# A softplus polynomial moved to GpSimd, the low mask products to ScalarE, and whole-chunk low halves on VectorE, in a two-layer hybrid decoder

## The chip, the cores and the metric

One Trainium2 chip, one of its cores. The metric is the device time of one execution in microseconds (us); the number given for a kernel is the median of several runs. Engines: TensorE (PE, its weight loads PEld), VectorE (DVE), ScalarE (ACT), GpSimd (POOL) and SyncE (SP), which issues the DMAs. Each engine takes its instructions strictly in the order in which they stand in its own queue.

## The reference

Two decoder layers on 256 tokens of width 1024 in float32. Each has a mixer (gated DeltaNet heads beside block attention heads, one output projection), a layer norm, a gated MLP with a causal convolution of width 3, and a layer norm. The part that the change touches is the log decay of the DeltaNet heads and how it becomes a decay matrix:

```python
beta = jax.nn.sigmoid(b_logit.astype(f32)).transpose(0, 2, 1)
g = (-jnp.exp(a_log.astype(f32)) * jax.nn.softplus(a_logit.astype(f32) + dt_bias.astype(f32))).transpose(0, 2, 1)
...
g = jnp.cumsum(g, axis=-1)
decay = jnp.exp(jnp.where(lower_incl, g[..., :, None] - g[..., None, :], -jnp.inf))
a_strict = jnp.where(idx[:, None] > idx[None, :],
                     jnp.einsum('bhncd,bhnmd->bhncm', k_beta, k) * decay, 0.0)
t_mat = a_strict + jnp.eye(c, dtype=q.dtype)
sol = lax.linalg.triangular_solve(t_mat, rhs, left_side=True, lower=True, unit_diagonal=True)
```

## The kernel before, in words

**Weights.** Every projection reads weights in chunks of 128x1024 float32. `load_raw` brings a chunk into one of 6 raw buffers `wr`. `split` makes two float32r halves of it: ScalarE copies the rounded high half `wh` (two 512-wide ops, L196), VectorE, or POOL where `le=pool`, subtracts it to get the low half `wl` (two 512-wide ops, L197). There are 5 buffers of each half. `proj` then runs 16 matmuls with the high half (L211 with the activations' high part, L212 with their low part) and 8 with the low half (L214) into a PSUM tile `pj`, of which there are two.

**A convolution chunk** (`u_conv`, names ka, qa, va): after `proj`, ScalarE scales `pj` by the last tap (L424), VectorE adds three taps from `pj` (L427, forms 255, 254, 253), ScalarE takes a tanh, VectorE forms the silu (L430). The `pj` tile is free for another chunk only after the last of the three VectorE taps. A rotary chunk (qb, kb) frees its `pj` by a ScalarE copy (L447).

**The decay.** `u_ab` projects the decay and beta logits, `u_ab2` (L390 to L418) forms y, beta, and the softplus as a chain of 128x8 operations: e = exp(-|y|), sd = e/(2+e) by a reciprocal, and a polynomial in sd squared, all on VectorE after the two exponentials. It ends in g, split into g_h and g_l, and in four products of a 128x512 triangular mask with them, `gx`: two with g_h on VectorE, two with g_l on POOL (L418). `u_decay` (L458 to L471) turns these by matmuls and exponentials into the decay matrices E0 and E1. `u_kk` and `u_sk` give k.k and its norms, `u_am` builds the matrix A on VectorE (L505, L507), which goes through DRAM to `u_solve`, a triangular solve of 28 small dependent POOL operations (L527, L529) and one copy, and back through DRAM to `gX` on VectorE (L543), which TensorE needs next (L560). `u_rp` adds the rotary part on POOL (L455, L456).

**Order.** The text table ORDER lists units (ab, ka:0, decay, ...) for each layer and, after @, engines on which a unit must stand after the one before it. Within these rules a scheduler with its own costs puts every engine's instructions in a fixed order. So an instruction that waits holds everything behind it on its engine.

**The MLP** runs for 22 column blocks of 128 two up-projection chunks and one down chunk of 128x1024 (12 matmuls of 512 columns); of the low halves of its up-projection, VectorE makes one chunk and POOL the other.

Of the kernel before, what the change touches and what calls it, by code (L numbers as in the profile page):

```python
# [11 lines left out]
F32 = mybir.dt.float32  # L12
F32R = mybir.dt.float32r
# [3 lines left out]
AF = mybir.ActivationFunctionType  # L17
OP = mybir.AluOpType
# [7 lines left out]
HG = 4  # L26
# [63 lines left out]
def hybrid_kernel(ctx, tc, xT, x, wab, wch, par, lnrow, cst, msk, out):  # L90
    nc = tc.nc
    pe, act, dve, pool, sp = nc.tensor, nc.scalar, nc.vector, nc.gpsimd, nc.sync
# [29 lines left out]
    def ps_a():  # L122
        return ac.tile([128, 512], F32, name="ac")
# [4 lines left out]
    m_le = kt[:, K_LE:K_LE + 128]  # L128
# [44 lines left out]
    def bc(ap, n):  # L173
        return ap[:, None, :].to_broadcast([128, n, 128])

    hold = {}
    nosync = mybir.DependencyInfo(mybir.DependencyClass.NoSync, mybir.DependencyReason.DATA)
# [6 lines left out]
    def split(raw, hp=None, le=None, tiles=None, cs=slice(0, 1024)):  # L184
        le = le or dve
        if tiles:
            h, lo = tiles
        elif hp is None:
            h = whp.tile([128, 1024], F32R, name="wh")
            lo = wlp.tile([128, 1024], F32R, name="wl")  # L190
        else:
            h = hp.tile([128, 1024], F32R, name="whh", bufs=N_HOLD)
            lo = hp.tile([128, 1024], F32R, name="wlh", bufs=N_HOLD)
        for q in range(cs.start, cs.stop, 512):
            s = slice(q, q + 512)
            ih = act.activation(h[:, s], raw[:, s], AF.Copy)  # L196
            il = le.tensor_tensor(lo[:, s], raw[:, s], h[:, s].bitcast(F32), op=OP.subtract)  # L197
            for i, e in ((ih, "act"), (il, "dve" if le is dve else "pool")):
                if e in hold:
                    tc.add_manual_dep(i.ins, hold[e].name, nosync, reason="norm first")  # L200
        return h, lo

    def load_chunk(l, ci, hp=None, le=None):
        return split(load_raw(l, ci), hp, le)
# [136 lines left out]
    for l in range(DEPTH):  # L341
# [5 lines left out]
        sh = [128, 2, HG]  # L347

        def sm(name):
            return small.tile(sh, F32, name=name, bufs=1)  # L350

        def mt(name, shape, bufs=1, dt=F32):
            return (early if name in EARLY else mix).tile(shape, dt, name=name, bufs=bufs)
# [4 lines left out]
        y, beta, ay, e, sd, s2, pl, g = (sm(n) for n in ("y", "beta", "ay", "e", "sd", "s2", "pl", "g"))  # L358
        sk, cj, ncj, rk, sq, so, wv = (sm(n) for n in ("sk", "cj", "ncj", "rk", "sq", "so", "wv"))
        g_h = small.tile(sh, F32R, name="g_h", bufs=1)  # L360
        g_l = small.tile(sh, F32R, name="g_l", bufs=1)
# [13 lines left out]
        G, T, st = [], {}, {}  # L375
# [15 lines left out]
        def u_ab2():  # L391
            ps = ps_a()
            for b in range(2):
                pe.matmul(ps[:, b * 8:b * 8 + 8], st["ab"][:, b * 128:b * 128 + 128], sel, start=True, stop=True)
            psv = ps[:, 0:16].rearrange("p (b c) -> p b c", b=2)
            dve.tensor_tensor(y, psv[:, :, 0:HG], pr[:, P_DT:P_DT + HG][:, None, :].to_broadcast(sh), op=OP.add)
            act.activation(beta, psv[:, :, HG:2 * HG], AF.Tanh, scale=0.5)
            dve.tensor_scalar(beta, beta, 0.5, 0.5, op0=OP.mult, op1=OP.add)
            dve.scalar_tensor_tensor(ay, y, -1.0, y, op0=OP.mult, op1=OP.max)
            act.activation(e, ay, AF.Exp, scale=-1.0)  # L400
            ea = small.tile([128, HG], F32, name="ea", bufs=1)
            act.activation(ea, pr[:, P_AL:P_AL + HG], AF.Exp)
            dve.tensor_scalar(sd, e, 2.0, None, op0=OP.add)
            dve.reciprocal(sd, sd)
            dve.tensor_tensor(sd, sd, e, op=OP.mult)
            dve.tensor_tensor(s2, sd, sd, op=OP.mult)
            dve.tensor_scalar(pl, s2, 2.0 / 17, None, op0=OP.mult)
            for n in (15, 13, 11, 9, 7, 5, 3):
                dve.scalar_tensor_tensor(pl, pl, 2.0 / n, s2, op0=OP.add, op1=OP.mult)
            dve.scalar_tensor_tensor(pl, pl, 2.0, sd, op0=OP.add, op1=OP.mult)  # L410
            dve.scalar_tensor_tensor(pl, y, 0.0, pl, op0=OP.max, op1=OP.add)
            dve.scalar_tensor_tensor(g, pl, -1.0, ea[:, None, :].to_broadcast(sh), op0=OP.mult, op1=OP.mult)
            dve.tensor_copy(g_h, g)
            dve.tensor_tensor(g_l, g, g_h.bitcast(F32), op=OP.subtract)
            for gg, eng in ((g_h, dve), (g_l, pool)):
                G.append(mt("gx", [128, 2, HG, 128], 2, F32R))
                for b in range(2):
                    eng.tensor_tensor(G[-1][:, b], bc(m_le, HG),  # L418
                                      gg[:, b, :].bitcast(F32)[:, :, None].to_broadcast([128, HG, 128]), op=OP.mult)

        def gdn_conv(ps, ct, dst):
            w = pr[:, P_GCONV + 4 * ct:P_GCONV + 4 * ct + 4]
# [359 lines left out]
        for item in (ORDER if isinstance(ORDER, str) else ORDER[l]).split():  # L782
            item, _, after = item.partition("@")
# [77 lines left out]
        held, held_w, fin = [], [], l == DEPTH - 1  # L861
# [12 lines left out]
        for j in range(2, FJ):  # L874
            cs = []
# [116 lines left out]
```

## Time and profile before

| what | value |
|---|---|
| median of 3 runs (lowest, highest) | 728.64 us (728.05, 730.34) |
| the profiled execution: its own time, its span | 728.23 us, 726.2 us |
| granted TensorE clock, mean over the span | 0.978 of full speed |
| busy: PE, PEld | 697.5 us (96%), 626.0 us (86%) |
| busy: DVE, ACT, POOL | 580.0 us (80%), 402.1 us (55%), 196.1 us (27%) |

The span runs from the first to the last instruction; 2.0 us of the execution's own time lie around it. By the lines that run, layer 0's mixer takes about 19 to 155 us and its MLP 186 to 350 us, layer 1's mixer 374 to 515 us and its MLP 543 to 708 us, with the norms between. A matmul of 256 columns starts 0.12 us after the one before it at full clock, so a chunk's 24 take 2.88 us; the "busy" of a matmul is longer than that since matmuls overlap. Idle time of an engine is listed with what ended it, so a TensorE row that ends in "<-DVE cv" waited for a VectorE tap.

### The profile page before, as it was taken

What the parts mean: (1) busy time and instruction counts of PE and PEld (TensorE: products, weight loads), DVE (VectorE), ACT (ScalarE), POOL (GpSimd) and SP (SyncE); (2) the same over time, 40 slices, a digit from 0 to 9 for tenths busy, and PEclk for the clock granted to TensorE, in tenths of its full rate; (3) what the DMA queues carried; (4) which work ended last, traced back from release to release, by engine and by line L of the source; (5) the groups of instructions that cost most, each with busy time, mean ns of one, the idle gap of its engine ahead of it and who ended that gap; (6) DMA issues with size and microseconds to landing.
All of it is one profiled execution on the core that took longest, in us unless ns stands there. A gap on an engine that the chain in (4) does not pass through costs nothing.

```text
span 726.2 us, 13935 instructions
## 1 busy us (share of the span) xinstructions
PE 697.5 (96%) x5184; PEld 626.0 (86%) x5184; DVE 580.0 (80%) x1285; ACT 402.1 (55%) x914; POOL 196.1 (27%) x200
## 2 busy tenths in 40 slices
PE   8988999999999999999999987999999999999994
PEld 5978888787899999999888986887779999999994
DVE  4899867599888888878879997576987888888756
ACT  5645456556666666665355453556466666666531
POOL 0146600004333333432002482000142433333412
PEclk9999989999999999999999996899999999999998
DMA  8866331531666765656153526044237666666201
GB/s 313 300 235 206 88 134 59 175 117 58 229 215 195 224 205 199 214 175 201 61 202 130 150 76 217 5 126 164 87 105 269 207 199 203 209 209 198 86 1 59
DMA packets 41218, 118.09 MB, mean 163 GB/s; under 512 B 10176, under 2 KB 12992, under 8 KB 40640
## 3 DMA queue, kind: packets, MB, share of 16 engines
q1 hardware_dynamic: 41152, 117.21, 48.8%
q8 instruction: 41, 0.67, 0.4%
q14 instruction: 25, 0.20, 0.1%
HBM read 114.84 MB, written 2.36 MB: 161 GB/s over the span
## 4 chain that ended last, share of the span: by engine, by line
PE 84%; DVE 7%; DMA 3%; POOL 2%; ACT 1%; issue 1%; SPq 0%; DVEq 0%; ACTq 0%
PE pj L211 15%; PE pj L212 15%; PE pj L214 14%; PE ac L722 8%; PE ac L723 8%; PE ac L721 8%; DVE wl L197 2%; PE pj L225 1%; PE pj L222 1%; PE pj L223 1%; PE mx L608 1%; PE mx L313 1%; POOL P L529 1%; DVE cv L427 1%; POOL T L527 1%
## 5 line engine op out<-in xcount | busy, mean ns | idle before, releaser
L196 ACT ACTIVATE wh<-wr 128x512 fp32r<-128x512 f32 x376 | 219.4, 622 | 99.2 <-PE pj L212 42.0
L211 PE MATMUL pj<-xh,wh 128*128 128x256 f32 x1024 | 258.9, 289 | 9.1 <-DVE cv L427 9.0
L212 PE MATMUL pj<-xl,wh 128*128 128x256 f32 x1024 | 257.4, 287 | 0.0
L197 DVE TENSOR_TENSOR wl<-wr,wh 128x512 fp32r<-128x512 f32 x292 | 208.8, 745 | 23.7 <-ACT wh L196 14.0
L211 PEld LDWEIGHTS pj<-xh,wh 128*128 128x128 f32 x1024 | 198.1, 193 | 13.6 <-issue 10.6
L212 PEld LDWEIGHTS pj<-xl,wh 128*128 128x128 f32 x1024 | 198.5, 194 | 1.7
L197 POOL TENSOR_TENSOR wl<-wr,wh 128x512 fp32r<-128x512 f32 x84 | 115.8, 1401 | 207.0 <-ACT wh L196 201.8
L214 PE MATMUL pj<-xh,wl 128*128 128x256 f32 x1024 | 147.3, 286 | 0.0
L214 PEld LDWEIGHTS pj<-xh,wl 128*128 128x128 f32 x1024 | 134.7, 195 | 0.0
L722 PE MATMUL ac<-wh,fal 128*128 128x512 f32 x144 | 56.4, 392 | 0.0
L721 PE MATMUL ac<-wh,fah 128*128 128x512 f32 x144 | 56.1, 392 | 0.0
L723 PE MATMUL ac<-wl,fah 128*128 128x512 f32 x144 | 56.0, 389 | 0.0
L831 DVE TENSOR_TENSOR fal<-fth,fah 128x256 fp32r<-128x256 f32 (+1 forms) x48 | 36.8, 767 | 17.3 <-ACT fah L830 17.0
L806 POOL TENSOR_SCALAR hw<-par 128x66 f32<-128x66 f32 x2 | 2.1, 1038 | 151.8 <-DVE wlh L197 151.8
L817 DVE SCALAR_TENSOR_TENSOR fc<-pj,par,fc 128x255 f32<-128x255 f32 x80 | 38.2, 477 | 4.2 <-ACT fc L813 2.8
L817 DVE SCALAR_TENSOR_TENSOR fc<-pj,hw,fc 128x255 f32<-128x255 f32 x80 | 38.4, 480 | 3.7 <-ACT fc L813 2.4
L828 DVE SCALAR_TENSOR_TENSOR fth<-fth,fc 128x256 f32<-128x256 f32 (+1 forms) x48 | 24.0, 499 | 20.1 <-ACT fth L827 20.1
L830 ACT ACTIVATE fah<-fth 128x256 fp32r<-128x256 f32 (+1 forms) x48 | 18.9, 394 | 36.4 <-DVE fth L829 36.4
L827 ACT ACTIVATE fth<-fc 128x256 f32<-128x256 f32 (+1 forms) x48 | 19.2, 401 | 35.7 <-DVE fc L817 35.4
L427 DVE SCALAR_TENSOR_TENSOR cv<-pj,par,cv 128x255 f32<-128x255 f32 (+2 forms) x72 | 34.0, 474 | 2.6 <-ACT cv L424 2.3
L723 PEld LDWEIGHTS ac<-wl,fah 128*128 128x128 f32 x144 | 27.0, 188 | 5.9
L721 PEld LDWEIGHTS ac<-wh,fah 128*128 128x128 f32 x144 | 27.2, 189 | 4.8
(257 smaller groups left out, 1065.1 us busy)
## 6 DMA issues: line engine op xcount, KB each, us to landing
wr<-in_wch_dram SPq DMA_DIRECT2D x195, 512.0 KB, 4.2
lnb<-in_lnrow_dram SPq DMA_DIRECT2D x4, 1024.0 KB, 5.3
xres<-in_x_dram SPq DMA_DIRECT2D x2, 512.0 KB, 6.1
da<-A SPq DMA_DIRECT2D x4, 256.0 KB, 2.5
ka<-in_wch_dram SPq DMA_DIRECT2D x2, 512.0 KB, 3.9
qa<-in_wch_dram SPq DMA_DIRECT2D x2, 512.0 KB, 5.1
qb<-in_wch_dram SPq DMA_DIRECT2D x2, 512.0 KB, 5.0
kb<-in_wch_dram SPq DMA_DIRECT2D x2, 512.0 KB, 5.8
```

Source lines behind the costliest of these rows:

```text
L196: ih = act.activation(h[:, s], raw[:, s], AF.Copy)
L197: il = le.tensor_tensor(lo[:, s], raw[:, s], h[:, s].bitcast(F32), op=OP.subtract)
L211: pe.matmul(ps, h[:, k, :], xh[:, k, :], start=k == 0, stop=False)
L212: pe.matmul(ps, h[:, k, :], xl[:, k, :], start=False, stop=False)
L214: pe.matmul(ps, lo[:, k, :], xh[:, k, :], start=False, stop=k == KT - 1)
L427: dve.scalar_tensor_tensor(cv[:, o:], ps[:, :S - o], w[:, j:j + 1], cv[:, o:], op0=OP.mult, op1=OP.add)
L721: pe.matmul(ps, a_h, w_h[:, ns], start=start and i == 0, stop=False, skip_group_check=True)
L722: pe.matmul(ps, a_l, w_h[:, ns], start=False, stop=False, skip_group_check=True)
L723: pe.matmul(ps, a_h, w_l[:, ns], start=False, stop=stop and i == len(items) - 1, skip_group_check=True)
L817: dve.scalar_tensor_tensor(cv[:, d], ps[:, d.start - o:d.stop - o], w[:, q:q + 1], cv[:, d], op0=OP.mult, op1=OP.add)
L828: dve.scalar_tensor_tensor(th, th, 1.0, cg[:, ts], op0=OP.add, op1=OP.mult)
L831: dve.tensor_tensor(al, th, ah.bitcast(F32), op=OP.subtract)
```

## The change

Three edits. In `u_ab2` all steps of the softplus from `sd*e` on go to POOL, where each multiply-add becomes two operations: 25 operations of 128x8 in place of 15 on VectorE. The two products with g_l leave POOL and become eight 128x128 ScalarE copies with a scale per partition; the two with g_h stay on VectorE. In `split`, a low half made by VectorE is one operation of 1024 columns, which needs both of ScalarE's 512-wide copies; POOL's stay at 512. (In the first chunk of the program, which is cut in two, the VectorE operations stay at 512.)

```diff
-        for q in range(cs.start, cs.stop, 512):
-            s = slice(q, q + 512)
-            ih = act.activation(h[:, s], raw[:, s], AF.Copy)
-            il = le.tensor_tensor(lo[:, s], raw[:, s], h[:, s].bitcast(F32), op=OP.subtract)
...
+        for s in [slice(q, q + 512) for q in range(cs.start, cs.stop, 512)]:
+            held(act.activation(h[:, s], raw[:, s], AF.Copy), "act")
+        w = cs.stop - cs.start if le is dve else 512
+        for s in [slice(q, q + w) for q in range(cs.start, cs.stop, w)]:
+            held(le.tensor_tensor(lo[:, s], raw[:, s], h[:, s].bitcast(F32), op=OP.subtract), "dve" if le is dve else "pool")
...
-            dve.tensor_tensor(sd, sd, e, op=OP.mult)
-            dve.tensor_tensor(s2, sd, sd, op=OP.mult)
-            dve.tensor_scalar(pl, s2, 2.0 / 17, None, op0=OP.mult)
+            pool.tensor_tensor(sd, sd, e, op=OP.mult)
+            pool.tensor_tensor(s2, sd, sd, op=OP.mult)
+            pool.tensor_scalar(pl, s2, 2.0 / 17, None, op0=OP.mult)
             for n in (15, 13, 11, 9, 7, 5, 3):
-                dve.scalar_tensor_tensor(pl, pl, 2.0 / n, s2, op0=OP.add, op1=OP.mult)
-            dve.scalar_tensor_tensor(pl, pl, 2.0, sd, op0=OP.add, op1=OP.mult)
-            dve.scalar_tensor_tensor(pl, y, 0.0, pl, op0=OP.max, op1=OP.add)
-            dve.scalar_tensor_tensor(g, pl, -1.0, ea[:, None, :].to_broadcast(sh), op0=OP.mult, op1=OP.mult)
-            dve.tensor_copy(g_h, g)
-            dve.tensor_tensor(g_l, g, g_h.bitcast(F32), op=OP.subtract)
-            for gg, eng in ((g_h, dve), (g_l, pool)):
-                G.append(mt("gx", [128, 2, HG, 128], 2, F32R))
-                for b in range(2):
-                    eng.tensor_tensor(G[-1][:, b], bc(m_le, HG),
-                                      gg[:, b, :].bitcast(F32)[:, :, None].to_broadcast([128, HG, 128]), op=OP.mult)
+                pool.tensor_scalar(pl, pl, 2.0 / n, None, op0=OP.add)
+                pool.tensor_tensor(pl, pl, s2, op=OP.mult)
+            pool.tensor_scalar(pl, pl, 2.0, None, op0=OP.add)
+            pool.tensor_tensor(pl, pl, sd, op=OP.mult)
+            pool.tensor_scalar(s2, y, 0.0, None, op0=OP.max)
+            pool.tensor_tensor(pl, pl, s2, op=OP.add)
+            pool.tensor_tensor(pl, pl, ea[:, None, :].to_broadcast(sh), op=OP.mult)
+            pool.tensor_scalar(g, pl, -1.0, None, op0=OP.mult)
+            pool.tensor_copy(g_h, g)
+            pool.tensor_tensor(g_l, g, g_h.bitcast(F32), op=OP.subtract)
+            G.extend(mt("gx", [128, 2, HG, 128], 2, F32R) for _ in range(2))
+            for b in range(2):
+                dve.tensor_tensor(G[0][:, b], bc(m_le, HG),
+                                  g_h[:, b, :].bitcast(F32)[:, :, None].to_broadcast([128, HG, 128]), op=OP.mult)
+                for h in range(HG):
+                    act.activation(G[1][:, b, h], m_le, AF.Copy, scale=g_l[:, b, h:h + 1].bitcast(F32))
```

The change also moves instructions, since the scheduler orders them anew. VectorE's queue in layer 0 around the products gx before (pl, g, g_h and g_l are steps of the softplus, cv is a convolution tap, sd the softplus's first quotient):

```order
L411 SCALAR_TENSOR_TENSOR pl<-y,pl 128x8
L197 TENSOR_TENSOR wl<-wr,wh 128x512
L412 SCALAR_TENSOR_TENSOR g<-pl,ea 128x8
L427 SCALAR_TENSOR_TENSOR cv<-pj,par_216,cv 128x255
L413 CAST g_h<-g 128x8
L197 TENSOR_TENSOR wl<-wr,wh 128x512
L414 TENSOR_TENSOR g_l<-g,g_h 128x8
L418 TENSOR_TENSOR gx<-kt,g_h 128x512 x2
```

The same queue and place now:

```order
L202 TENSOR_TENSOR wl<-wr,wh 128x1024
L437 SCALAR_TENSOR_TENSOR ka<-th,cv 128x256
L406 RECIPROCAL sd<-sd 128x8
L434 SCALAR_TENSOR_TENSOR cv<-pj,par_213,cv 128x255
L202 TENSOR_TENSOR wl<-wr,wh 128x1024
L434 SCALAR_TENSOR_TENSOR cv<-pj,par_213,cv 128x254
L202 TENSOR_TENSOR wl<-wr,wh 128x1024
L423 TENSOR_TENSOR gx<-kt,g_h 128x512 x2
L434 SCALAR_TENSOR_TENSOR cv<-pj,par_213,cv 128x253
L456 STREAM_SHUFFLE sw<-qb 128x256
```

Between the reciprocal and gx there stood 31 rows before, now four; the last tap (253) of the second convolution chunk, which stood ahead of gx, stands right behind it. In layer 1, where 30 rows stood between them, one low half, one silu and two taps do now, and again a 253 tap stands behind gx.

TensorE's queue in layer 1, behind the third chunk, before (ac<-ka are k.k products):

```order
L214 MATMUL pj<-xh,wl 128x256 x8
L494 MATMUL ac<-ka 128x256
L495 MATMUL ac<-ka 128x128
L211 MATMUL pj<-xh,wh 128x256
L212 MATMUL pj<-xl,wh 128x256
```

and now:

```order
L216 MATMUL pj<-xh,wl 128x256 x8
L501 MATMUL ac<-ka 128x256
L502 MATMUL ac<-ka 128x128
L469 MATMUL ac<-gx,gt_r 128x512 x2
L470 MATMUL ac<-gx,gt_r 128x512
L213 MATMUL pj<-xh,wh 128x256
L214 MATMUL pj<-xl,wh 128x256
```

Three of the four decay matmuls that read gx moved ahead of the fourth and fifth chunk; before they stood behind both. In layer 0 they stay behind the fifth chunk.

ScalarE's queue in layer 0 at the new products:

```order
L199 ACTIVATE wh<-wr 128x512 x4
L454 ACTIVATE qb<-pj 128x256
L426 ACTIVATE gx<-kt,g_l 128x128 x8
L436 ACTIVATE th<-cv 128x256
L431 ACTIVATE cv<-pj,par_213 128x256
```

The eight products are new there, behind the copy that frees a `pj` tile and ahead of the next convolution's tanh and first tap.

## Rows read from the trace of the kernel before

**Rows 1.** Page, chain that ended last, shares of the span by engine.
```profile
PE 84%; DVE 7%; DMA 3%; POOL 2%; ACT 1%; issue 1%; SPq 0%; DVEq 0%; ACTq 0%
```

**Rows 2.** Busy time by stretch: PE, PEld, DVE, ACT, POOL, then clock, DMA share, GB/s.
```profile
20.00:155.00 135.00, 129.40 (x1170) 115.41 (x1168) 110.45 (x303) 75.72 (x207) 32.10 (x48) 0.96 0.49 163
186.00:350.00 164.00, 163.95 (x1165) 154.58 (x1165) 132.13 (x236) 102.41 (x209) 52.81 (x38) 1.00 0.64 209
```

**Rows 3.** Busy time, same columns, of the stretch around layer 0's decay.
```profile
30.00:50.00 20.00, 17.77 (x130) 16.29 (x129) 19.78 (x66) 10.01 (x22) 6.83 (x6) 1.00 0.73 265
```

**Rows 4.** Waits: who waited for whom, us in total, times, longest.
```profile
ACT wh L196 <- PE pj L212: 42.0, 36, 2.8
...
PE pj L211 <- DVE cv L427: 9.0, 7, 2.2
```

**Rows 5.** Timeline of VectorE, layer 0: start, us, instruction, idle before it.
```profile
21.83 2.48 DVE L197 TENSOR_TENSOR wl<-wr,wh 128x512 fp32r<-128x512 f32 x4
...
26.48 0.19 DVE L404 RECIPROCAL sd<-sd 128x8 f32<-128x8 f32 x1
...
29.52 0.16 DVE L409 SCALAR_TENSOR_TENSOR pl<-pl,s 128x8 f32<-128x8 f32 x1
29.60 0.68 DVE L197 TENSOR_TENSOR wl<-wr,wh 128x512 fp32r<-128x512 f32 x1
...
30.28 0.47 DVE L427 SCALAR_TENSOR_TENSOR cv<-pj,par,cv 128x253 f32<-128x253 f32 x1
...
35.62 2.13 DVE L418 TENSOR_TENSOR gx<-kt,g_h 128x512 fp32r<-128x512 f32 x2
```

**Rows 6.** Timeline of VectorE, layer 1.
```profile
381.95 0.20 DVE L404 RECIPROCAL sd<-sd 128x8 f32<-128x8 f32 x1
...
390.53 2.13 DVE L418 TENSOR_TENSOR gx<-kt,g_h 128x512 fp32r<-128x512 f32 x2
...
437.81 3.49 DVE L197 TENSOR_TENSOR wl<-wr,wh 128x512 fp32r<-128x512 f32 x1
```

**Rows 7.** Timeline of POOL, layer 1's solve (28 dependent steps) and rotary part.
```profile
420.17 0.60 POOL L527 TENSOR_TENSOR T<-T,P 64x14 f32<-64x14 f32 x1 [1.20 <-DVE P L524]
420.85 1.82 POOL L529 TENSOR_TENSOR P<-P,T 64x14 f32<-64x14 f32 x1
...
435.46 0.23 POOL L527 TENSOR_TENSOR T<-T,P 64x26 f32<-64x26 f32 x1
435.76 0.24 POOL L529 TENSOR_TENSOR P<-P,T 64x26 f32<-64x26 f32 x1
...
436.92 0.21 POOL L529 TENSOR_TENSOR P<-P,T 64x14 f32<-64x14 f32 x1
...
437.95 1.43 POOL L455 TENSOR_TENSOR sw<-sw,kt 128x256 f32<-128x256 f32 x2
```

**Rows 8.** Timeline of TensorE: where chunks and gX matmuls begin.
```profile
33.77 0.28 PE L211 MATMUL pj<-xh,wh 128*128 128x256 f32 x1
...
39.74 0.36 PE L211 MATMUL pj<-xh,wh 128*128 128x256 f32 x1 [1.36 <-DVE cv L427]
...
386.15 0.39 PE L211 MATMUL pj<-xh,wh 128*128 128x256 f32 x1
...
394.64 0.36 PE L211 MATMUL pj<-xh,wh 128*128 128x256 f32 x1 [0.31 <-DVE cv L427]
...
446.04 1.32 PE L560 MATMUL ac<-gX,A 32*32 32x16 f32 x32 [2.36 <-DVE gX L543]
```

**Rows 9.** Busy time and clock, columns of Rows 2, layer 1 around the solve.
```profile
424.00:426.00 2.00, 0.31 (x3) 0.11 (x1) 1.97 (x5) 0.59 (x2) 1.76 (x4) 1.00 0.22 88
...
442.00:444.00 2.00, 1.67 (x7) 1.38 (x7) 0.21 (x1) 1.17 (x3) 0.00 (x0) 0.50 0.95 106
...
458.00:460.00 2.00, 2.00 (x16) 1.87 (x16) 0.48 (x1) 1.51 (x3) 0.00 (x0) 0.78 0.00 0
```

**Rows 10.** Groups of ScalarE by form: a 128x128 operation's mean ns.
```profile
L477 ACT ACTIVATE scr<-ac 128x128 bf16<-128x128 f32 x16 | 4.4, 277 | 7.6 <-PE ac L476 7.6
```

More of the change, by code (lines that the diff above doesn't have):

```diff
@@ L193, in split, with held @@
             lo = hp.tile([128, 1024], F32R, name="wlh", bufs=N_HOLD)
-        for q in range(cs.start, cs.stop, 512):
-            s = slice(q, q + 512)
-            ih = act.activation(h[:, s], raw[:, s], AF.Copy)
-            il = le.tensor_tensor(lo[:, s], raw[:, s], h[:, s].bitcast(F32), op=OP.subtract)
-            for i, e in ((ih, "act"), (il, "dve" if le is dve else "pool")):
-                if e in hold:
-                    tc.add_manual_dep(i.ins, hold[e].name, nosync, reason="norm first")
+        def held(i, e):
+            if e in hold:
+                tc.add_manual_dep(i.ins, hold[e].name, nosync, reason="norm first")
+        for s in [slice(q, q + 512) for q in range(cs.start, cs.stop, 512)]:
[3 more added lines that the diff above has]
+            held(le.tensor_tensor(lo[:, s], raw[:, s], h[:, s].bitcast(F32), op=OP.subtract), "dve" if le is dve else "pool")
         return h, lo
```

## The prediction

> **What bounds the kernel now.** I read the page's chain first: 84% of the span is TensorE, 7% VectorE, 2% POOL [rows 1]. The stretches then tell where that 7% lies. In layer 0's MLP TensorE is busy 163.95 of 164 us while VectorE has 132.13 [rows 2]: nothing that VectorE saves there can shorten it. In the mixer TensorE is busy 129.40 of 135, and around the decay, 30 to 50 us, VectorE is busy 19.78 of 20 while TensorE has 17.77 [rows 3]. So the decay is a place where VectorE sets the pace. The waits say through what: TensorE waits 9.0 us in all, seven times, for a convolution's last tap, which frees a `pj` tile; ScalarE mostly waits for TensorE to give a `wh` buffer back, so it runs several chunks ahead [rows 4]. Layer 1 has a second limit behind the decay: TensorE waits 2.36 us for gX, the end of the solve, and its clock is at half speed from about 442 to 459 us [rows 8, 9].
>
> **What VectorE loses as work.** An 8-column step lasts 0.16 us, but the next operation starts 0.08 after it [rows 5]; 15 steps leave per layer, 1.2 us. The two products with g_h take 2.13 us beside POOL's two, against 0.68 for a 512-wide operation that runs alone [rows 5]; with POOL's gone I count 1.3, so 0.8 saved. A merged low half saves at most the part of an operation that its successor sees, 0.08 us, since even an 8-column one costs that; it saves at least nothing. Seven or so chunks pass during the decay: up to 0.6 us. Together about 2.6 us per layer at this place.
>
> The Trainium skill (VectorE: DVE Perf Modes, "The TRN2 errata") gives (N+151)/0.96 ns for a float32 tensor_tensor of N columns, and says that one large tile pays the fixed part once. That is 691 ns for 512 columns, and the single operation here agrees (0.68 us [rows 5]). By that rule a merge would save 157 ns; but four operations take 2.48 us [rows 5], so each starts 0.60 after the one before and half of the fixed part is already hidden. By the rule the sum below would be about 1 us lower in all.
>
> **What POOL gains as latency.** This is the term that decides. The nearest rows are the solve's: dependent POOL steps, undisturbed 0.30 us from start to start (435.46, 435.76), over all 28 steps 17.0 us, 0.61 each [rows 7]. The difference is VectorE: a step of 14 columns lasts 1.82 us where VectorE runs one two-input operation after another [rows 7], and in turn one VectorE low half lasts 3.49 us while POOL's rotary operations run [rows 6, 7]. So POOL steps wait for such VectorE operations. g_h is the chain's 24th step. Bounds: 24 x 0.25 = 6 us (shorter operations, none held up) and 24 x 0.61 = 14.6 us. I take 0.30 x 24 = 7.2 us plus the VectorE low halves that the new order puts beside it, since VectorE then stands idle and holds nothing up.
>
> **The queues.** The scheduler has put gx only four VectorE rows behind the reciprocal. VectorE will stand at gx, with the second convolution's last tap behind it, and with that tap a `pj` tile.
>
> Layer 0. The reciprocal ended at 26.67 [rows 5]; a whole low half stands ahead of it now, so 27.8. The chain: 7.2, plus two low halves of 1.2, plus the masks' cast, which now stands inside the chain (0.7, like a rotary operation [rows 7]): g_h at 38.1. VectorE's four rows take 0.4 + 1.2 + 0.4 + 1.2 (a tap's 0.47 less the overlap, twice 0.60 [rows 5]): it is done at 31.0 and idle for 7.1 us. Then gx (1.3) and the tap (0.4): 39.8. The fifth chunk needs that tile; it began at 33.77 [rows 8] and will begin 6.0 us later. Part of that comes back, since before, the sixth chunk was itself held up (39.74, idle 1.36 [rows 8]). By VectorE's count the loss is 7.1 less 2.6, or 4.5; by TensorE's, the fifth chunk ends at 42.7, the decay's matmuls no longer wait, and the sixth waits for the fourth's taps: behind 39.8 VectorE still has a shuffle, two norm sums, a product and a silu (1.6), three taps (1.2) and two low halves (2.4), so until 45.0, where it began at 39.74 with 1 us of decay matmuls inside it: 4.2 late. I take **+4**.
>
> Layer 1. The reciprocal ended at 382.15 [rows 6]; half a low half more stands ahead: 382.6. The chain: 7.2, plus a low half and a silu, 1.6: g_h at 391.4, VectorE idle from 385.0, 6.4 us. TensorE reaches its moved gx matmuls where it began the fourth chunk, 386.15 [rows 8], and stands until the tap at 393.1. Then come two chunks (5.8) and three decay matmuls (0.7): the sixth chunk begins at 399.6 instead of 394.64 [rows 8], 4.9 late. The matrix A and so the solve move by what VectorE lost, 6.4 less 2.6, or 3.8; TensorE's 2.36 us for gX absorb some of the difference [rows 8]. I take **+3.5**.
>
> ScalarE's eight products: at most 8 x 0.277 = 2.2 us [rows 10], beginning one step after g_h and so ending about a microsecond behind VectorE's. Behind them wait a tanh, a first tap and high halves; the halves are covered by the lead over TensorE [rows 4], the taps are in the counts above. If that lead were gone, 2 us per layer. The raw buffer of the masks is given back some 4 us later; the same lead covers it.
>
> **The clock.** With TensorE busy 0.31 of 2 us (424 to 426) it stayed full; in 442 to 444 it was at half, until about 459 [rows 9]. Two new waits of 6 us each can drop it. Below: nothing. Above: 17 us at half again, up to 8 each. Near nothing is likelier, since dense chunks follow these waits, not more waits, and VectorE limits them anyway: **+1** each.
>
> **Elsewhere** the mixers' some 25 other merged chunks each save VectorE up to 2.0 us per layer, which counts only where VectorE is behind: **-1** per layer. In the MLP nothing.
>
> Sum: 4 + 3.5 + 2 - 2 = +7.5 us on the profiled execution's 728.23: 735.7. The median of the runs is 0.4 above that execution, so **736.1 us**.
>
> **Rivals.** (1) *The chain is quick enough, and the kernel is faster.* At 0.25 us a step with nothing held up, g_h comes at 34.5 and 388.6, VectorE idles 3.5 us each time, and the 2.6 us saved and a merge or two more cover nearly all of it; then the 2 us of the other chunks remain: 728.6 - 2 = 726.6. For it: the shortest rows; against it: low halves beside the chain in both layers, and POOL steps that have waited for them [rows 7]. The point that decides is g_h within about 3.5 us of the end of what stands ahead of gx. 0.12. (2) *The wait moves and heals.* TensorE arrives late at gX, no longer idles there, and the half-speed stretch of 17 us in layer 1 [rows 9] shrinks; it gives back up to half of it, 8 us: 728. Nothing says which way that goes. 0.12. (3) *POOL runs at the solve's mean.* 0.61 a step: 7.4 us more a layer, less the hold-ups counted already (2.4 and 1.6): +5.0 and +5.8, so 747. Against it, VectorE idles. 0.08. (4) *Long low halves collide in the MLP.* POOL's pairs hold a 1024-wide one as in Rows 6, the taps behind come too late for two `pj` tiles: 0.1 us in each of 40 blocks, 740. Against: 32 us of spare VectorE time there [rows 2]. 0.04.
>
> **Chances.** The forecast 0.64, between 731 and 742: each layer's loss by bounds of 2 to 7, the clock 0 to 5. All measured against 728.64; a change under 0.3%, 2.2 us, can't be told from none. Faster: two thirds of rival 1, a quarter of rival 2: 0.11. Same: the rest of these, and forecasts whose losses fall to 1 us a layer: 0.16. Slower 0.73. The range for 8 in 10: 728 to 743; about 0.12 lies below and 0.07 above.
>
> **What would show it.** VectorE idle 5 to 7 us ahead of gx in each layer, ended by POOL; TensorE idle about as long ahead of the fifth chunk (layer 0) and the gx matmuls (layer 1); 24 POOL steps in 9 to 10 us; MLP stretches of unchanged length; a 1024-wide low half of about 1.2 us. The forecast is wrong if POOL's steps take under 0.2 us, if VectorE doesn't idle at gx, or if the mixers end no later than before.

## The result, and the profile after

The changed kernel took 745.87 us (median of 4 runs, 739.51 to 753.60) against 728.35 for the kernel before beside it; the ratio is 1.0157, 95% interval 1.0117 to 1.0197, or 11.4 us. Ratios here and below leave out runs more than 1.5% above the fastest of the same kernel (here 751.19 and 753.60 us), so this one is smaller than the ratio of the medians. Run again with the experiments (e1, below) it took 742.70 against 726.55: 1.0222, 1.0191 to 1.0252, or 16.1 us. The forecast was slower by 7.5, range 728 to 743. The direction was right and the size too small: by its ratio the first result is 739.8 us, and the median of e1 is 742.70, both inside the range but near its upper end (745.87 lies above it).

The first profile of the changed kernel (span 751.8) has TensorE at half clock from 104 to 124 us; the second profile (e1, span 739.9) has little of that, and I read the second from here on. Busy time by stretch, first profile:

```profile
104.00:124.00 20.00, 20.00 (x242) 16.25 (x240) 8.30 (x29) 6.26 (x22) 0.00 (x0) 0.50 0.01 2
```

The same view of the second profile, with the stretches of [rows 2, 3]; the clock is the third number from the end:

```profile
20.00:155.00 135.00, 126.22 (x1146) 113.53 (x1144) 102.02 (x249) 73.75 (x209) 37.10 (x71) 0.95 0.48 159
186.00:350.00 164.00, 163.40 (x1155) 153.44 (x1155) 133.08 (x192) 101.34 (x205) 54.17 (x39) 1.00 0.63 206
30.00:50.00 20.00, 14.34 (x92) 13.27 (x91) 13.37 (x26) 10.06 (x25) 8.49 (x25) 0.83 0.64 214
...
104.00:124.00 20.00, 19.81 (x270) 16.97 (x267) 12.38 (x39) 11.89 (x42) 0.00 (x0) 0.91 0.16 55
```

The MLP stretch reads as before [rows 2]. Around the decay, 30 to 50 us, VectorE was busy 19.78 us before [rows 3] and is busy 13.37 now, and TensorE lost 3.43 us of its 17.77. So VectorE, which set the pace there, now waits. The waits of the second profile, TensorE's and then VectorE's, say for what (us in total, times, longest):

```profile
PE pj L213 <- DVE cv L434: 12.2, 6, 5.1
PE ac L469 <- DVE gx L423: 5.6, 1, 5.6
...
DVE gx L423 <- POOL g_h L419: 11.8, 2, 6.1
```

VectorE stands at gx for GpSimd's g_h, twice, 11.8 us in all; TensorE stands behind VectorE, once at a convolution's tile and once at gx. The chain that ended last hardly shows it; its shares by engine are close to [rows 1], with ScalarE at 4% instead of 1%:

```profile
PE 84%; DVE 7%; ACT 4%; POOL 2%; issue 2%; DMA 2%; SPq 0%; DVEq 0%; ACTq 0%
```

VectorE's timeline, layer 0 (start, us, instruction, idle before it), to be read beside [rows 5]:

```profile
27.41 0.20 DVE L406 RECIPROCAL sd<-sd 128x8 f32<-128x8 f32 x1
27.74 0.48 DVE L434 SCALAR_TENSOR_TENSOR cv<-pj,par,cv 128x255 f32<-128x255 f32 x1
28.14 1.22 DVE L202 TENSOR_TENSOR wl<-wr,wh 128x1024 fp32r<-128x1024 f32 x1
29.27 0.48 DVE L434 SCALAR_TENSOR_TENSOR cv<-pj,par,cv 128x254 f32<-128x254 f32 x1
29.66 1.22 DVE L202 TENSOR_TENSOR wl<-wr,wh 128x1024 fp32r<-128x1024 f32 x1
37.03 1.30 DVE L423 TENSOR_TENSOR gx<-kt,g_h 128x512 fp32r<-128x512 f32 x2 [6.14 <-POOL g_h L419]
38.25 0.47 DVE L434 SCALAR_TENSOR_TENSOR cv<-pj,par,cv 128x253 f32<-128x253 f32 x1
```

GpSimd's chain beside it:

```profile
28.05 0.20 POOL L408 TENSOR_TENSOR s<-sd 128x8 f32<-128x8 f32 x1
28.34 1.12 POOL L409 TENSOR_SCALAR pl<-s 128x8 f32<-128x8 f32 x1
29.54 0.25 POOL L411 TENSOR_SCALAR pl<-pl 128x8 f32<-128x8 f32 x1
29.87 1.07 POOL L412 TENSOR_TENSOR pl<-pl,s 128x8 f32<-128x8 f32 x1
31.03 0.23 POOL L411 TENSOR_SCALAR pl<-pl 128x8 f32<-128x8 f32 x1
31.35 0.20 POOL L412 TENSOR_TENSOR pl<-pl,s 128x8 f32<-128x8 f32 x1
...
34.25 0.72 POOL L167 CAST km<-wr 128x640 uint8<-128x640 f32 x1
...
36.80 0.20 POOL L419 CAST g_h<-g 128x8 fp32r<-128x8 f32 x1
```

A free step starts 0.28 to 0.33 us after the one whose result it needs. The two that met a 1024-wide low half lasted 1.12 and 1.07, and they ended 0.10 and 0.06 behind that low half (29.46 and 30.94, against 29.36 and 30.88). VectorE has nothing left to do ahead of gx: from 30.9 it stands until 37.03. The Trainium skill (SBUF — State Buffer, "Terms") says that the port pair of VectorE and GpSimd is held for a whole instruction and that the loser blocks fully; these two steps agree.

TensorE's timeline, the chunks and matmuls of [rows 8]:

```profile
38.77 0.58 PE L213 MATMUL pj<-xh,wh 128*128 128x256 f32 x1 [5.10 <-DVE cv L434]
...
45.06 0.47 PE L213 MATMUL pj<-xh,wh 128*128 128x256 f32 x1
...
396.98 1.47 PE L469 MATMUL ac<-gx,gt_r 128*128 128x512 f32 x2 [5.59 <-DVE gx L423]
...
406.54 0.47 PE L213 MATMUL pj<-xh,wh 128*128 128x256 f32 x1
```

Where the time went, from rows of the timelines: layer 0's mixer up to the MLP's first transposes on TensorE (`ac<-kt,fu`, 175.23 before, 180.09 now) lost 4.9 us; the MLP behind it, up to layer 1's y on VectorE (380.22, 384.70), gained 0.4; layer 1's mixer, from y to its MLP's first transposes (532.76, 546.12), lost 8.9; the rest lost 0.3. I use these two lengths of the mixers for the experiments too.

### The profile page after: what moved, and what is told of

It is laid out like the page before. It is cut to its first block, busy times and chain, and to the rows that moved or that the text cites. A ratio compares the mean times of both kernels' runs of the same rounds, so it can differ in the third digit from the quotient of the medians.

```text
span 751.8 us, 13848 instructions
## 1 busy us (share of the span) xinstructions
PE 716.7 (95%) x5184; PEld 639.1 (85%) x5184; DVE 574.7 (76%) x1094; ACT 405.3 (54%) x930; POOL 204.5 (27%) x246
## 4 chain that ended last, share of the span: by engine, by line
PE 80%; DVE 9%; ACT 3%; DMA 3%; issue 2%; POOL 2%; SPq 0%; DVEq 0%; ACTq 0%
PE pj L213 15%; PE pj L214 14%; PE pj L216 13%; PE ac L728 7%; PE ac L730 7%; PE ac L729 7%; DVE wl L202 3%; DMA wr<-in_wch_dram 3%; ACT wh L199 2%; PE mx L615 2%; DVE fc L824 1%; PE mx L315 1%; DVE cv L434 1%; PE pj L227 1%; PE mx L658 1%
## 5 line engine op out<-in xcount | busy, mean ns | idle before, releaser
L213 PE MATMUL pj<-xh,wh 128*128 128x256 f32 x1024 | 263.4, 293 | 13.2 <-DVE cv L434 11.8
L214 PE MATMUL pj<-xl,wh 128*128 128x256 f32 x1024 | 260.0, 289 | 0.0
L202 DVE TENSOR_TENSOR wl<-wr,wh 128x1024 fp32r<-128x1024 f32 (+1 forms) x147 | 192.2, 1312 | 37.4 <-ACT wh L199 26.9
L213 PEld LDWEIGHTS pj<-xh,wh 128*128 128x128 f32 x1024 | 201.2, 196 | 19.4 <-issue 9.7
L214 PEld LDWEIGHTS pj<-xl,wh 128*128 128x128 f32 x1024 | 201.6, 197 | 1.5
L202 POOL TENSOR_TENSOR wl<-wr,wh 128x512 fp32r<-128x512 f32 x84 | 118.0, 1426 | 206.6 <-ACT wh L199 206.6
L216 PE MATMUL pj<-xh,wl 128*128 128x256 f32 x1024 | 149.3, 288 | 0.0
L838 DVE TENSOR_TENSOR fal<-fth,fah 128x256 fp32r<-128x256 f32 (+1 forms) x48 | 39.7, 826 | 13.9 <-ACT fah L837 13.9
```

What stands on the lines that cost most here:

```text
L202: held(le.tensor_tensor(lo[:, s], raw[:, s], h[:, s].bitcast(F32), op=OP.subtract), "dve" if le is dve else "pool")
L213: pe.matmul(ps, h[:, k, :], xh[:, k, :], start=k == 0, stop=False)
L214: pe.matmul(ps, h[:, k, :], xl[:, k, :], start=False, stop=False)
L216: pe.matmul(ps, lo[:, k, :], xh[:, k, :], start=False, stop=k == KT - 1)
L838: dve.tensor_tensor(al, th, ah.bitcast(F32), op=OP.subtract)
```

## The experiments

My theory at the start: the loss is VectorE standing at gx behind a slow GpSimd chain, with TensorE behind it and the clock falling (theory 1). The rivals: the wide low halves or ScalarE's products make most of it (2); the chain's latency costs wherever the products stand (3).

| run | what it is | ratio to before (95%) | layer 0 mixer | layer 1 mixer |
|---|---|---|---|---|
| e1 | changed kernel again | 1.0222 (1.0191 to 1.0252) | +4.9 | +8.9 |
| e2 | chain alone | 1.0144 (1.0122 to 1.0167) | +4.8 | +3.7 |
| e3 | wide low halves alone | 1.0185 (1.0119 to 1.0250) | +5.7 | +2.7 |
| e4 | changed, products behind | 1.0168 (1.0109 to 1.0227) | +10.5 | +3.0 |
| e5 | ScalarE's products alone | 0.9996 (0.9979 to 1.0013) | +0.8 | -2.4 |
| e6 | changed, narrow low halves | 1.0140 (1.0114 to 1.0166) | +6.5 | +2.5 |
| e7 | e6, products behind | 0.9987 (0.9970 to 1.0005) | +2.5 | -1.8 |
| e8 | changed, waits filled | 1.0274 (1.0213 to 1.0334) | +7.7 | +6.4 |
| e9 | changed, TensorE's order back | 1.0203 (1.0164 to 1.0241) | +13.9 | +10.6 |
| e10 | before, wide from chunk 11 | 1.0022 (0.9994 to 1.0049) | +0.7 | +1.6 |
| e11 | e7 in layer 1 alone | 0.9977 (0.9961 to 0.9994) | +1.3 | -3.0 |
| e12 | all three edits, mended | 1.0023 (0.9999 to 1.0047) | -0.9 | +6.5 |

The two last columns are of each run's single profile, in us against the kernel before. They scatter by a microsecond or two: e11 leaves layer 0 as it was before and reads +1.3 there. The profiles of e4, e9 and e12 (runs of 742.35, 752.74 and 734.38 us) hold a long stretch at half clock (last section), in e4 and e9 in layer 0, in e12 in layer 1; it is in these columns. Each edit also lets the scheduler order all queues anew, so a row prices an edit together with its order.

**e1, the changed kernel again.**

> The changed kernel once more, to have a second profile of it and a closer ratio. Both theories: 8 to 15 us above the kernel before. What is open in it is how much of the loss lies in the two waits at the mask products (5.1 us and 5.6 us of TensorE in the first profile) and how much in stretches at half clock behind them and further on: if the half-clock stretch from 102 to 130 us comes with the change it is there again; if it is a disturbance of that one execution, the stretch is as short as before the change (about 7 us) and the layer 0 loss up to the first MLP falls from 14.6 to about 7 us.

It was 16 us slower, a little outside what I wrote; the long half-clock stretch was not there, and layer 0's mixer lost 4.9 us, where it lost 14.5 in the first profile. At TensorE's first matmuls behind layer 0's solve (`ac<-T,gx`) the two profiles are still alike, 6.6 and 7.1 us late; what differs behind that point is the clock. Layer 1's mixer lost 9.0 in the first profile, 8.9 in this one.

**e2, the chain alone.** Only the block of after's lines 407 to 420 is taken over.

```diff
-            dve.tensor_tensor(sd, sd, e, op=OP.mult)
+            pool.tensor_tensor(sd, sd, e, op=OP.mult)
...
-            dve.tensor_tensor(g_l, g, g_h.bitcast(F32), op=OP.subtract)
+            pool.tensor_tensor(g_l, g, g_h.bitcast(F32), op=OP.subtract)
```

> The kernel before with only the softplus chain on GpSimd; both mask products where they were, low halves in two operations. Theory 1 (VectorE stands at the mask products behind a slow GpSimd chain, TensorE behind it, and the clock falls): the whole loss is here, 8 to 14 us slower, VectorE idle 5 to 7 us ahead of gx in each layer. Theory 2 (the wide low halves or ScalarE's products make most of it): 0 to 4 us slower.

1.0144, or 10.5 us, with VectorE idle at gx for 4.95 and 4.36 us, a little less than I wrote: by itself it looked as if theory 1 held and the rest was small.

**e3, the wide low halves alone.**

```diff
-            il = le.tensor_tensor(lo[:, s], raw[:, s], h[:, s].bitcast(F32), op=OP.subtract)
...
+        w = cs.stop - cs.start if le is dve else 512
+        for s in [slice(q, q + w) for q in range(cs.start, cs.stop, w)]:
+            held(le.tensor_tensor(lo[:, s], raw[:, s], h[:, s].bitcast(F32), op=OP.subtract), "dve" if le is dve else "pool")
```

> The kernel before with only the low halves of VectorE's chunks in one operation of 1024 columns. Theory 1: 0 to 2 us faster, since some 32 merges a layer's mixer save about 0.07 us each on VectorE, and only where VectorE is late; in the MLPs nothing. Theory 2 (a chunk's first half is ready later and long operations hold GpSimd up): 2 to 5 us slower, with longer MLP stretches.

1.0185, or 13.4 us (three of the four runs lie at 736.1 to 737.8, some 10 us above before, one at 745.6): the part that I had counted as a saving costs about as much as the chain. The MLP did not get longer (204.92 us from transposes to y, before 204.99), so it is not the collision that my rival 4 has in the MLP. VectorE's timeline in layer 0 of this run, between the reciprocal (27.27) and g_h:

```profile
28.07 1.22 DVE L202 TENSOR_TENSOR wl<-wr,wh 128x1024 fp32r<-128x1024 f32 x1
...
33.53 1.21 DVE L202 TENSOR_TENSOR wl<-wr,wh 128x1024 fp32r<-128x1024 f32 x1
...
34.74 1.22 DVE L202 TENSOR_TENSOR wl<-wr,wh 128x1024 fp32r<-128x1024 f32 x1
...
36.94 1.22 DVE L202 TENSOR_TENSOR wl<-wr,wh 128x1024 fp32r<-128x1024 f32 x1
38.07 0.16 DVE L415 CAST g_h<-g 128x8 fp32r<-128x8 f32 x1
38.14 0.47 DVE L429 SCALAR_TENSOR_TENSOR cv<-pj,par,cv 128x253 f32<-128x253 f32 x1
```

and TensorE's:

```profile
38.76 0.36 PE L213 MATMUL pj<-xh,wh 128*128 128x256 f32 x1 [2.34 <-DVE g_l L416]
...
41.18 0.79 PE L465 MATMUL ac<-gx,gt_r 128*128 128x512 f32 x1 [1.24 <-POOL gx L420]
```

Before, five operations of half a chunk stood in that place, 0.60 each from start to start; now four whole chunks do, 1.13 each, and another ahead of the reciprocal. That is 1.5 us more work between the reciprocal and g_h of a chain that grew by 2.4 (8.4 to 10.8). g_h comes at 38.07 instead of 34.88, and the mask products behind it as late. The chunks do not begin late here: the tap at 38.14, which frees the sixth chunk's tile, now stands ahead of gx, and the sixth chunk begins at 38.76, where it began at 39.74 before [rows 8]. What is late is the rest of it. The kernel before, g_h, GpSimd's two products and the sixth chunk's last eight matmuls:

```profile
34.88 0.16 DVE L413 CAST g_h<-g 128x8 fp32r<-128x8 f32 x1
...
35.78 2.87 POOL L418 TENSOR_TENSOR gx<-kt,g_l 128x512 fp32r<-128x512 f32 x2 [3.74 <-DVE g_l L414]
...
42.63 1.12 PE L214 MATMUL pj<-xh,wl 128*128 128x256 f32 x8
```

The same products and matmuls in e3, and the busy time and clock around them:

```profile
38.77 4.34 POOL L420 TENSOR_TENSOR gx<-kt,g_l 128x512 fp32r<-128x512 f32 x2 [5.88 <-DVE g_l L416]
...
46.34 1.77 PE L216 MATMUL pj<-xh,wl 128*128 128x256 f32 x8
...
41.00:47.00 6.00, 5.51 (x19) 4.09 (x20) 3.58 (x4) 0.43 (x1) 2.10 (x2) 0.50 0.57 197
```

GpSimd's products start 3.0 us later and last 4.34 instead of 2.87, beside low halves that last 1.67; TensorE stands at them for 1.24 and 0.31 us inside the sixth chunk, and from 41 to 47 us its clock is at half (0.50, before 1.00). The last eight matmuls begin 3.7 us late. Half a low half is a small thing to stand behind; a whole one is not. How much of the 3.7 is the waits and how much the clock was not tested.

**e4, the products moved back in the queue.** The products become a unit of their own, placed in the order string behind ka:3 in layer 0 and behind ka:2 in layer 1.

```diff
+        def u_gx():
             G.extend(mt("gx", [128, 2, HG, 128], 2, F32R) for _ in range(2))
...
-... ka:3@G ka:1 kk:0 decay@AGD ...
+... ka:3@G gx@D ka:1 kk:0 decay@AGD ...
-... ka:2@G ka:1@P kk:0 decay@ADG ...
+... ka:2@G gx@D ka:1@P kk:0 decay@ADG ...
```

> The changed kernel with one thing moved: VectorE's products with g_h stand about a dozen rows further back in its queue, behind the last taps of the convolutions that TensorE waits for, and ScalarE's eight behind a tanh and a first tap; the chain stays on GpSimd with its latency. Theory 1 (the loss is the place of the products in the queue, not the chain's latency in itself): TensorE's wait of about 5 us ahead of the fifth chunk goes, and with it the half-clock stretch, in each layer; the kernel comes to between 2 us faster and 3 us slower than before. Theory 3 (the latency itself is the loss: the decay matrices come too late wherever the products stand): the wait reappears at the decay's matmuls or the solve, 6 us slower or more.

TensorE's wait of 5 us ahead of the fifth chunk went, and VectorE's at gx fell to 1.65 us in layer 0, as theory 1 has it; but the kernel stayed 12 us slower, the size that theory 3 forecast. Theory 3's wait at the decay's matmuls is there, but it is small: 1.63 us in layer 0, 0.87 before. At TensorE's first matmuls behind the solve (`ac<-T,gx`) layer 0 is 3.2 us late and layer 1, counted from y, 1.3 us early, where e1 is 6.6 and 7.5 late; the rest is lost behind the solves, in layer 0 at half clock (0.50 from 100 to 125 us, before 0.92). The four runs differ too: 734.0, 735.5, 742.4 (the profiled one) and 742.6. The wide low halves are still there, so with e3 they were the next thing to take away.

**e5, ScalarE's products alone.**

```diff
-            for gg, eng in ((g_h, dve), (g_l, pool)):
+            for b in range(2):
+                dve.tensor_tensor(G[0][:, b], bc(m_le, HG), ...)
+                for h in range(HG):
+                    act.activation(G[1][:, b, h], m_le, AF.Copy, scale=g_l[:, b, h:h + 1].bitcast(F32))
```

> The kernel before with only the products with g_l on ScalarE; the chain and its short steps on VectorE, low halves in two operations. The first runs gave the chain alone 1.4% and the wide low halves alone 1.9% slower, both together 2.2%, so they do not add. Theory 1 (each of those two costs by itself, the products nothing): within 2 us of before, and VectorE's two products with g_h fall from 2.1 us to about 1.3. Rival (ScalarE's eight products delay the tanh and the taps behind them): 3 to 6 us slower.

No difference that can be measured. VectorE's two products take 1.28 us instead of 2.13 [rows 5], since GpSimd no longer runs its own beside them.

**e6 and e7, narrow low halves, with the products in front and behind.** e6 is the changed kernel with one line back; e7 adds the edit of e4.

```diff
-        w = cs.stop - cs.start if le is dve else 512
+        w = 512
```

> The changed kernel with the low halves in two operations of 512 again: chain on GpSimd, products with g_l on ScalarE. Theory 1 (chain and wide low halves each cost some 10 us through the same place, the convolutions' last taps ahead of the fifth and sixth chunk, and overlap there): about as slow as the chain alone, 8 to 12 us above before. If they were independent, this would give back the 13 us that the wide ones cost alone: 0 to 5 us above before.

> As the run before, with the products with g_h moved some dozen rows further back in VectorE's queue, behind the last taps. Theory 1 (two separate causes: the place of the products in the queue, and the wide low halves): with both taken away the loss goes, within 3 us of before, no half-clock stretch between 36 and 47 us. Theory 3 (the chain's latency on GpSimd costs wherever the products stand): 5 us slower or more.

e6: 10.2 us, as the chain alone. e7: nothing, 0.9987. So there are two causes, each enough for some 10 us, which overlap: with either left in, the loss stays; with both out, it goes. In the changed kernel itself the wide low halves make some 6 us of the loss (e1's 16.1 less e6's 10.2); as ScalarE makes the products with g_l there, GpSimd's long pair of e3 is not how. Theory 3 falls, and clearly. GpSimd's chain in e7:

```profile
29.47 0.74 POOL L412 TENSOR_TENSOR pl<-pl,s 128x8 f32<-128x8 f32 x1
30.30 0.23 POOL L411 TENSOR_SCALAR pl<-pl 128x8 f32<-128x8 f32 x1
...
33.30 0.76 POOL L411 TENSOR_SCALAR pl<-pl 128x8 f32<-128x8 f32 x1
34.14 0.49 POOL L412 TENSOR_TENSOR pl<-pl,s 128x8 f32<-128x8 f32 x1
...
38.45 0.48 POOL L419 CAST g_h<-g 128x8 fp32r<-128x8 f32 x1
```

Because VectorE keeps working, more steps are held up, and the chain takes 11.0 us (27.92 to 38.93) where in e1 it took 9.2. The slower chain belongs to the faster kernel.

**e8, the waits filled.** 20 matmuls of zeros ahead of the fifth chunk in layer 0 and ahead of the fourth in layer 1.

```diff
+        def u_wm(n):
+            ps = ps_m()
+            for _ in range(n):
+                pe.matmul(ps, warm[:, 0:128], warm, start=True, stop=True)
...
-... ka:3@G ka:1 kk:0 decay@AGD ...
+... ka:3@G wm:20@P ka:1@P kk:0 decay@AGD ...
-... qb:0@P ka:2@G ka:1@P kk:0 ...
+... qb:0@P wm:20@P ka:2@G ka:1@P kk:0 ...
```

> The changed kernel with 20 matmuls of zeros (128x512, bf16, into a free PSUM tile that nothing reads) on TensorE where it stands still before the fifth chunk of layer 0, and 20 ahead of the fourth chunk of layer 1; they take about 4.5 us each time and lie inside the wait. If the clock's fall behind the wait is a cost of its own (about half of a 7 us stretch each time), the kernel becomes 3 to 7 us faster than the changed kernel and the half-clock stretches behind the two waits go. If the clock is not a cost (VectorE is the limit there anyway), within 1.5 us of it.

TensorE's timeline, layer 0:

```profile
33.27 4.26 PE L469 MATMUL mx<-zero 128*128 128x512 bf16 x19
38.29 0.39 PE L213 MATMUL pj<-xh,wh 128*128 128x256 f32 x1 [0.75 <-DVE cv L435]
...
44.48 0.35 PE L213 MATMUL pj<-xh,wh 128*128 128x256 f32 x1 [1.66 <-DVE cv L435]
```

The half-clock stretch behind the wait is gone: the fifth chunk's last eight matmuls begin at 40.31, against 42.35 in e1. But the sixth chunk, which in e1 begins at 45.06 without a wait, now waits 1.66 us for a tap and begins at 44.48, only 0.6 earlier. In layer 1, counted from y, the chunk behind the wait was 2.2 us earlier than in e1 and the sixth 0.8 (its last eight matmuls). No tap held the sixth there: the zeros had also changed TensorE's order, which now has k.k products and the rest of the matmuls on gx ahead of that chunk. The three taps of the fourth chunk, and then the sixth chunk:

```profile
405.24 1.50 DVE L435 SCALAR_TENSOR_TENSOR cv<-pj,par,cv 128x255 f32<-128x255 f32 x3
...
408.30 0.47 PE L213 MATMUL pj<-xh,wh 128*128 128x256 f32 x1
```

The taps end 2.1 us earlier than in e1, counted from y, and the sixth chunk begins 1.6 us behind them. The kernel did not get faster (lowest run 742.57, in e1 740.09), so 3 to 7 us was wrong. In layer 0 the clock behind the wait is not where the loss lies, since the taps hold the sixth chunk anyway. In layer 1, whose mixer is 2.4 us shorter than in e1, this run does not settle it.

**e9, TensorE's order put back in layer 1.** In layer 1 only the three edits together made the scheduler move the gx matmuls ahead of two chunks (in e6 it did so in layer 0).

```diff
-... ka:2@G ka:1@P kk:0 decay@ADG ...
+... ka:2@G ka:1@P kk:0 decay@PADG ...
```

> The changed kernel with TensorE's matmuls on gx in layer 1 held behind the convolutions' chunks (an order edge on TensorE; VectorE, ScalarE and GpSimd as in the changed kernel). Only the three edits together made the scheduler move these matmuls ahead of the fourth and fifth chunk, and layer 1's mixer lost 9 us, where the chain alone and the wide low halves alone lost 3 to 4 each. Theory 1 (the extra loss of layer 1 is TensorE standing at the moved matmuls): 4 to 6 us faster than the changed kernel, the wait of 5.6 us at the gx matmul gone. Rival (VectorE's late taps limit there, whatever TensorE's order): within 2 us of the changed kernel.

The rival was right: 1.0203, as e1 within the intervals. TensorE's timeline, layer 1:

```profile
406.99 0.55 PE L213 MATMUL pj<-xh,wh 128*128 128x256 f32 x1 [6.66 <-DVE cv L434]
```

The wait of 5.6 us at gx became one of 6.7 at the fourth chunk's tile: VectorE's tap stands behind gx, whatever TensorE runs first.

**e10, wide low halves from the eleventh chunk on.** A list that is empty at a layer's start is filled at its first u_rp; the low half is one operation only when it is filled (138 merges of 161), on the kernel before.

```diff
+        w = cs.stop - cs.start if le is dve and wide else 512
...
         def u_rp():
+            wide.append(1)
```

> The kernel before with low halves in one operation of 1024 from the eleventh chunk of each layer on (138 merges instead of 161), and in two operations up to there, through the convolutions around the decay. Theory 1 (wide low halves cost only where taps and the short chain wait behind them, ahead of the decay): within 2 us of before, perhaps 1 us faster. Rival (they cost throughout the mixer and the MLP, by later first halves or by holding GpSimd up): 5 us slower or more.

1.0022, 0.9994 to 1.0049: no loss, so the loss of e3 lies in its other 23 merges, around the decay. And no gain: VectorE's busy time is 580.1 us with these merges, 580.0 with all of them, and 580.0 before.

**e11 and e12.** e11 is the kernel before in layer 0 and e7 in layer 1; e12 has all three edits, with e4's place for the products and e10's rule for the low halves.

```diff
+            if l == 0:
+                dve.tensor_tensor(sd, sd, e, op=OP.mult)
...
+                return
             pool.tensor_tensor(sd, sd, e, op=OP.mult)
```

> A try at a version that beats both kernels: layer 0 as before; in layer 1 the chain on GpSimd, products with g_l on ScalarE, products with g_h some rows further back in VectorE's queue; low halves in two operations. With both layers so, layer 1's mixer was 1.8 us shorter and layer 0's 2.5 longer. Theory 1: 1 to 2.5 us faster than before. Rival (the 1.8 us of layer 1 were the clock's scatter in one profile): no difference.

> All three edits kept, each where it costs nothing by theory 1: chain on GpSimd and products with g_l on ScalarE, products with g_h behind the last taps, low halves in one operation from the eleventh chunk of each layer on. Theory 1: within 2 us of before, so some 13 us faster than the changed kernel. If the wide low halves cost elsewhere too: 5 us slower or more.

e11 is the only version that beats before: 0.9977, 0.9961 to 0.9994, or 0.4 to 2.8 us. As one interval of twelve that just misses 1, that is weak evidence. e12 is within 2 us of before (1.0023) and about 14 us faster than the changed kernel. In its profile TensorE's first matmuls behind layer 1's solve (`ac<-T,gx`) come 4.8 us earlier than before, counted from y; the mixer then loses 11.3 us against before, at half clock for 35 us, where before had some 17 [rows 9]:

```profile
445.00:480.00 35.00, 35.00 (x341) 28.96 (x341) 14.82 (x44) 12.70 (x46) 0.00 (x0) 0.51 0.17 61
```

## Why the prediction was right, and where it was not

**GpSimd's latency: right.** I took 0.30 us a step; it was 0.28 to 0.33. Hold-ups by the two low halves: 2.4 forecast, 1.7 measured (1.12 and 1.07 less two free steps). The masks' cast stood inside the chain with 0.72, as counted. g_h was done at 37.0, forecast 38.1; in layer 1 the chain took 8.2 us behind the reciprocal, forecast 8.8. ScalarE's eight products took 2.46 us, not at most 2.2, and ended some 2 us behind VectorE's, not one; e5 shows no cost of them.

**The queue and layer 0: right.** VectorE idle 6.1 (forecast 7.1), the tap done at 38.7 (39.8), fifth chunk 38.8 (39.8), sixth 45.1 (45.0), layer 0's mixer +4.9; the forecast for it was +4, +1 for the clock and -1 for the merges. I had counted both engines here, and they come out close together: in e1 the taps behind gx end at 44.8, and TensorE is busy up to the sixth chunk, with the fifth at half clock and then the decay's matmuls. With TensorE quick (e8) the chunk waits for the taps. That the sum fits is in part luck, since the -1 had the wrong sign (below).

**Layer 1: the term that was mis-sized, +3.5 forecast and +8.9 measured** (with +1 and -1 beside it, as in layer 0). VectorE idle was 5.6 (forecast 6.4), so the wait was not the error. Counted from y, the sixth chunk began 7.4 us late, not 4.9, and the matrix A on VectorE came 7.5 late, not 3.8. A before, and in e1:

```profile
404.13 0.49 DVE L505 SCALAR_TENSOR_TENSOR A<-ac,ncj,E 128x256 f32<-128x256 f32 x1
...
416.15 0.48 DVE L512 SCALAR_TENSOR_TENSOR A<-ac,ncj,E 128x256 f32<-128x256 f32 x1
```

Two steps failed. First, I let TensorE run two chunks and the decay's matmuls at full clock from the end of the wait. In e1 the clock is down there (0.66 on average from 392 to 402 us): three matmuls on gx and the fourth chunk take from 396.98 to 403.16, 6.2 us, where I had counted 3.6. These 2.6 us are about the difference at the sixth chunk. Second, I credited VectorE with 2.6 us of saved work behind the wait. It did not get to use them, as the timelines of ScalarE and VectorE in e1 show, beside TensorE's fifth chunk:

```profile
402.41 1.16 ACT L199 ACTIVATE wh<-wr 128x512 fp32r<-128x512 f32 x2 [2.36 <-PE pj L214]
...
403.16 0.28 PE L213 MATMUL pj<-xh,wh 128*128 128x256 f32 x1
...
403.59 1.23 DVE L202 TENSOR_TENSOR wl<-wr,wh 128x1024 fp32r<-128x1024 f32 x1 [2.52 <-ACT wh L199]
```

VectorE stood 2.5 us for a high half, and ScalarE 2.4 us for the buffer of it, which TensorE, late and at half clock, had not given back. So the lead of ScalarE over TensorE [rows 4], which I named as the cover, did not cover this. Nor did TensorE's old wait at gX absorb anything: it is gone in e1, but from A to TensorE's first matmuls behind the solve it took 46.3 us before and 46.3 in e1.

**The merged low halves: the wrong sign, and hidden by the sum.** I wrote that a merge "saves at least nothing" and took 1 us a layer. Alone they cost 13.4 us (e3), around the decay; elsewhere 138 of them bring nothing (e10). I had looked at the cost of the operation and not at who stands behind it: it is ready only when both high halves are, and it is placed as a whole ahead of taps and chain steps. The error hardly shows in layer 0's sum, because there the two edits hold up the same chunk, the sixth: its last eight matmuls begin 3.8 us late with the chain alone (46.47 in e2), 3.7 with the wide low halves alone (46.34 in e3) and 4.5 with both (47.16 in e1), and the mixer loses 4.8, 5.7 and 4.9. In layer 1 they add: A is 6.2 and 1.5 us late alone and 7.5 together. Behind A the chain alone makes up 2.5 of that and the changed kernel nothing, so the mixer loses 3.7 and 2.7 alone and 8.9 together; why it makes up nothing I did not settle.

The Trainium skill's formula for a float32 tensor_tensor (VectorE: DVE Perf Modes, "The TRN2 errata") gives an estimate of 1224 ns for 1024 columns, and the trace agrees (1.22 us). The saving of 157 ns a merge, my estimate from the same section's rule that one large tile pays the fixed part once, does not show: two halves cost 1.20 from start to start and one whole 1.13, and VectorE's busy time stayed at 580 us.

**The clock: +1 was about right in layer 0** (0.6 at the sixth chunk, e8). In layer 1 the half clock took the 2.6 us of TensorE's time named above; e8 gave 0.8 of it back at the sixth chunk, in another order, so its price there stays open. What I did not foresee is the scatter behind the solve (last section).

**The rivals.** (1) fell: VectorE idled 6 us. (2) fell in e1: TensorE no longer waits at gX, but its clock around the solve is on average what it was (0.85 from 424 to 480 us before, 0.85 from 436 to 492 in e1). e12 shows the mechanism with the sign turned: an earlier solve met a longer stretch at half clock. (3) fell: 0.38 us a step with all hold-ups, not 0.61. (4) fell in the MLP (204.6 us, before 205.0), but its idea, long low halves and GpSimd's pairs that hold each other up, is what e3 shows in the mixer (the pair of products took 4.34 us, before 2.87).

## What to carry to other kernels

A chain moved to a slower idle engine costs its latency only where something stands behind its consumer in an in-order queue: move the consumer behind the work that others wait for (here a dozen rows) and even a slower chain is free. An operation that is made larger to save a fixed cost is also a longer thing to stand behind; look for the short urgent operations around it before counting the saving, and merge only where nobody waits. And when two edits delay the same chunk, neither each alone nor both together shows their prices: take each of them away, and then both.

## What the hardware showed beyond that

A GpSimd step of 8 columns that meets a low half on VectorE lasts until that low half is done: 1.07 to 1.26 us beside 1024 columns (e1, e4), up to 0.76 beside 512 (e7, layer 0). A convolution's tap, which reads one of its two tiles (`pj`) from PSUM, did not hold such a step up: at 30.30 in e7 one took its free 0.23 us beside a tap from 30.07 to 30.55. On VectorE, merging 161 pairs of 512-wide operations left its busy time as it was.

TensorE's clock behind layer 0's solve differs between two profiles of one kernel. From 104 to 124 us it was 0.50 in the first profile of the changed kernel, in e4 and in e9, and between 0.83 and 1.00 before and in e1, e2, e3, e5, e6, e7, e8, e10 and e11; e12 had the long stretch in layer 1 instead, 35 us at 0.51. These four kernels have wide low halves, and no profile of a kernel without them shows it; but e1, which is the changed kernel itself, e3, e8 and e10 have them too and do not show it. The times point the same way: from the lowest to the highest run, kernels with wide low halves spread by 4.4 to 15.3 us, the others by 2.3 to 5.9, and four of e10's ten runs (730.7 to 739.1) lie above all 29 of the kernel before beside it (725.2 to 730.2). So merges away from the decay may cost something in some executions, which the ratios of e10 and e12 do not show. What starts the long stretch was not tested and stays open.
